# Seven products instead of eight for the first pair of K tiles in a feed-forward, and one low part instead of two

## The chip, the core and the metric

The kernel runs on one core of one Trainium2 chip. The metric is device time of one execution in microseconds (us); the median of three runs is given, with the lowest and highest. A core has five engines that take their own instructions in order: TensorE (PE, matrix products), VectorE (DVE), ScalarE (ACT), GpSimd (POOL, used here only to issue DMAs) and SyncE (SP, which issues most loads). They meet through semaphores: an instruction waits until another engine or a DMA has counted far enough.

## The reference

One block of an encoder, in float32, on 256 tokens of width 2048:

```
x += 1/2 * swiglu(norm(x))         # first feed-forward, inner width 5632
x += gated merge of two recurrent branches of norm(x), through w_out
x += cross attention to 256 memory tokens
x += 1/2 * swiglu(norm(x))         # second feed-forward
return norm(x)

def swiglu(h, w_up, w_down):
    gate, up = split(h @ w_up, 2)
    return (silu(gate) * up) @ w_down
```

The change touches the `h @ w_up` of the first feed-forward, and in one detail that of the second as well. There h is 256 x 2048 and w_up 2048 x 11264; gate and up are its two halves.

## The kernel before, in words

**Split operands.** A float32 matrix product of full accuracy is made of three faster ones. Each operand is split into a high part `h` (the value rounded to the type fp32r, made by ACT with a copy) and a low part `l` (value less high part, made by DVE with a subtraction): function `split`. A product is high times high, low of x times high of w, and high of x times low of w: function `three`, lines 547, 548 and 550. The x operands are the stationary side, 128 x 128; the weights stream past, 512 columns at a time.

**Groups and pairs.** The inner width of a feed-forward is worked through in 11 groups of 512 (g from 0 to 10). In a group the 2048 rows of x and w_up are taken as eight pairs of 128-row K tiles, p from 0 to 7; the weights of one pair are one load of 128 x 2048: two K tiles times gate and up. After the eight pairs the group is evacuated from PSUM (`ev`), multiplied, turned by transposes into `hidop`, and used in a later group by the down products (`wd`, four loads of 128 x 2048 in a group from g = 3 on).

**Seven products.** With two K tiles, two halves of the tokens, and gate and up, a pair is a 2 x 2 by 2 x 2 block product. Written out (kind "plain") it takes eight products of a 128 x 128 block of x with 512 columns of w, each three matmuls. Kind "fast" takes Strassen's scheme in Winograd's form: seven products, 21 matmuls, of sums and differences of blocks. For this the weights need four more blocks, `td`, made by DVE in three operations (L285, L287, L288), and split like the others into `th` and `tl`; x needs four sums as well, made once by `operand_pairs` and kept in the second half of the slots `xh` and `xl`. Kind "mixed" leaves w as it is and puts differences of x in its place: eight products, 24 matmuls, and the results still land in the seven accumulators of "fast". The x differences of "mixed" are the operand `less`. The table `PRODUCTS` lists, for each product, block of x, block of w and accumulator.

**Order.** `ffn_order` writes the order of pairs and down products by hand. From the fourth group on (g of 3 and more) nearly all pairs are fast; p0 is mixed, because the second half of its `xh` and `xl` holds `less` and has no room for the sums. `BOTH` lists those pairs of x that have both `less` and sums; for these, `less` stands in extra tiles, `xd`.

**Preparing weights.** `weights` takes items from the plan two ahead of their use and calls `prepare`, which loads, makes `td`, and splits. For p3 to p6 of groups 4 and up (function `adds`) the low part of the weights is not made by DVE: ACT writes the negated high part source (L293) and POOL issues a DMA that adds the weights to it (L294). Two dictionaries, `head` and `rest`, hang other work behind the preparation of numbered items: the operands of x, residual loads, sums.

**Buffers and scheduler.** Loads have three buffers (`raw`), high parts three (`h`), low parts three (`l`); `td`, `tl` and the evacuated `ev` of the first feed-forward share three of `wide`. The second feed-forward has no such pool for `tl`, two more load buffers, and loads most of its `td` ready-made from HBM, where the middle of the kernel has put them (`make_ahead`, tile `prep`). The order of instructions on each engine comes from a scheduler that places them by its own costs and the program's priorities; `tc.issue_after` binds some of them to a place. So a change in the program can move instructions that it does not name.

Of the kernel before, what the change touches and what calls it, by code (L numbers as in the profile page):

```python
# [8 lines left out]
F32 = mybir.dt.float32  # L9
F32R = mybir.dt.float32r  # L10
ACT = mybir.ActivationFunctionType
ALU = mybir.AluOpType

P = 128
# [27 lines left out]
def ffn_order(every=False):  # L42

    out = [(("mixed" if p > 5 else "fast") if every else "plain", 0, p) for p in range(8)]
    down = [("down", 0, 1, c, 0) for c in range(4)]  # L50
    for g in range(1, NG):
        if every:
            out += [("fast", g, p) for p in (1, 3, 4, 0, 2, 5, 6, 7)]
        elif g < 3:
            out += [(("mixed", "fast")[p % 2], g, p) for p in (0, 1, 2, 3, 5, 4, 7, 6)]
        else:
            out += [("mixed" if p == 0 or g == 3 and p == 6 else "fast", g, p)
                    for p in ((1, 3, 0, 4, 2, 6, 5, 7) if g == 3 else (1, 3, 4, 0, 2, 5, 6, 7))]
        if g > 2 and g % 2:
            down = [("down", g - 2, 2, c, b) for c in range(4) for b in (g - 2, g - 1)]  # L60
        n = 2 if g < 3 else 4
        out, down = out + down[:n], down[n:]
    return out + [("down", NG - 2, 2, c, b) for c in range(4) for b in (NG - 2, NG - 1)]
# [14 lines left out]
def block_kernel(ctx: ExitStack, tc: tile.TileContext, xT, xin, memT, vec, gfin, bgate, lruw, wu1, wd1, win, wv,  # L78
                 wg, wab, wout, wq, wk, wvm, wo, wu2, wd2, out_):
    nc = tc.nc  # L80
    pe, dve, act, sp = nc.tensor, nc.vector, nc.scalar, nc.sync
# [23 lines left out]
    def slot(dt=F32, name="slot"):  # L105
        return slots.tile([P, 1024], dt, name=name, tag="slot")
# [24 lines left out]
    x = [xt[k // 4][:, (k % 4) * T:(k % 4 + 1) * T] for k in range(KT)]  # L131
    ident = col("ident", 0, P)

    done = {}


    def split(h, l, raw):
        done["high"] = act.activation(h, raw, ACT.Copy).ins  # L138
        done["low"] = dve.tensor_tensor(out=l, in0=raw, in1=h.bitcast(F32), op=ALU.subtract).ins  # L139

    def split_tiles():
        return hp.tile([P, 2048], F32R, name="h", tag="h"), lp.tile([P, 2048], F32R, name="l", tag="l")


    plan, ahead, made_ahead = [], [], []
    orders = {"ffn1": ffn_order(), "ffn2": ffn_order(every=True)}

    def plan_ffn(name, wu, wd):
# [41 lines left out]
    head, rest = [], {}  # L190
# [29 lines left out]
    def weights(*key):  # L220
        while plan and len(ahead) < 2:
            i = next(planned)
            k, src, kind = plan.pop(0)
            if i == 0:
                in_turn.enter_context(tc.manual_schedule(engines={sp.engine, act.engine, dve.engine}))
            if i < len(head):
                head[i]()
            if plan and plan[0][2] == "added":
                begun.append(begin_added(plan[0][1]))
            ahead.append((k, prepare(src, kind, 4 if i < 4 else 1)))  # L230
            if i in rest:
                rest[i]()
            beside(i)
            if i == 7:
                in_turn.close()
        k, w = ahead.pop(0)
        assert k == key, (k, key)
        return w
# [4 lines left out]
    def raw_tile():  # L243

        if "raw2" in scoped and next(loads) % 5 > 2:
            return scoped["raw2"].tile([P, 2048], F32, name="raw2", tag="raw2")
        return rawp.tile([P, 2048], F32, name="raw", tag="raw")
# [10 lines left out]
    def prepare(src, kind, cuts=1):  # L258

        if kind == "added":  # L260
            raw, l = begun.pop(0)
            h = hp.tile([P, 2048], F32R, name="h", tag="h")
            done["high"] = act.activation(h, raw, ACT.Copy).ins
            return h, l
        raw = raw_tile()
        n = 2048 // cuts
        if kind == "plain":
            h, l = split_tiles()
            for a in range(0, 2048, n):
                sp.dma_start(raw[:, a:a + n], src[:, a:a + n])  # L270
                split(h[:, a:a + n], l[:, a:a + n], raw[:, a:a + n])
            return h, l
        if kind == "ready":
            src, t = src
            sp.dma_start(raw[:, 512:], src[:, 512:])
            td = raw_tile()
            sp.dma_start(td, t)
        else:
            sp.dma_start(raw, src)
            if "raw2" in scoped:  # L280
                td = raw_tile()
            else:
                td = scoped["wide"].tile([P, 2048], F32, name="td", tag="wide")
            two = [v[:, a:a + 1024].rearrange("p (i n) -> p i n", i=2) for v, a in ((td, 0), (raw, 512))]
            dve.tensor_tensor(out=two[0], in0=raw[:, None, :512].broadcast_to([P, 2, 512]), in1=two[1],  # L285
                              op=ALU.subtract)
            dve.tensor_tensor(out=td[:, 1024:1536], in0=raw[:, 1024:1536], in1=td[:, :512], op=ALU.subtract)  # L287
            dve.tensor_tensor(out=td[:, 1536:], in0=raw[:, 1536:], in1=td[:, 1024:1536], op=ALU.subtract)  # L288
        h, l = split_tiles()
        if kind != "fast added":  # L290
            split(h[:, 512:], l[:, 512:], raw[:, 512:])
        else:
            act.activation(l[:, 512:], raw[:, 512:], ACT.Copy, scale=-1.0)  # L293
            nc.gpsimd.dma_start(l[:, 512:], src[:, 512:], accum_op=ALU.add)  # L294
            done["high"] = act.activation(h[:, 512:], raw[:, 512:], ACT.Copy).ins
        th = hp.tile([P, 2048], F32R, name="h", tag="h")
        if "wide" in scoped:
            tl = scoped["wide"].tile([P, 2048], F32R, name="tl", tag="wide")
        else:
            tl = lp.tile([P, 2048], F32R, name="tl", tag="l")  # L300
        for a in (0, 1024):
            split(th[:, a:a + 1024], tl[:, a:a + 1024], td[:, a:a + 1024])
        return (h, l), (th, tl)

    def product(xs, *ws, late=()):
# [182 lines left out]

    BOTH = [2, 4, 6]
    xd = []

    def operand_pairs(src, gain, q, xg, out, every=False):


        for a in src:
# [8 lines left out]
            if every:  # L506
                less = None
                if q == 3:
                    if not i:
                        xd.append(slot(F32R, "xd"))  # L510
                    less = [xd[-1][:, a:a + 256] for a in (512 * i, 512 * i + 256)]
            elif 2 * q + i in BOTH:
                n = 512 * (BOTH.index(2 * q + i) % 2)
                if not n:
# [4 lines left out]
        def sums(which=((0, "less"), (0, "sums"), (1, "less"), (1, "sums"))):  # L519
            s = slot(name="xs")  # L520
            for i, ((h, l), less) in enumerate(out):
                a = [xg[:, i * 512 + j * P:][:, :P] for j in range(4)]

                def made(h, l, n, at, terms):
                    o = [s[:, at + j * P:][:, :P] for j in range(n)]
                    for j, (x, y, op) in enumerate(terms(o)):
                        dve.tensor_tensor(out=o[j], in0=x, in1=y, op=op)
                    split(h, l, s[:, at:at + n * P])

                if less and (i, "less") in which:  # L530
                    made(*less, 2, 0, lambda o: ((a[0], a[1], ALU.subtract), (a[2], a[3], ALU.subtract)))
                if (every or i or 2 * q in BOTH) and (i, "sums") in which:
                    if not every and not i and len(which) > 1:
# [139 lines left out]
    pairs1, sq1 = [], TokenSquares()  # L673
# [30 lines left out]
    def late_sums(q):  # L704
        with tc.issue_after(done["low"]):
            sums1[q](((0, "sums"),))

    for q, i in ((1, 16), (2, 17), (3, 26)):
        rest[i] = lambda q=q: late_sums(q)


    par = const.tile([P, 96], F32, name="par")
# [56 lines left out]
    xs = xs2.tiles  # L769
# [372 lines left out]
    for g in range(4):  # L1142
# [4 lines left out]
        for t in range(2):  # L1147
            s = slot(F32R, "vs")
# [8 lines left out]
    for h in range(HEADS):  # L1157
        for j in range(4):
            acc = bank()
            for t in range(2):  # L1160
                ps = probs[h][:, t * 512:(t + 1) * 512]
                s = vs[h, t]
# [153 lines left out]
```

## Time and profile before

| | us |
|---|---|
| median of three runs | 2428.28 (2426.31 to 2430.49) |
| span of the profiled execution, first to last instruction | 2425.5 |
| PE busy in the span | 2409.3 (99%) |
| DVE busy | 2025.6 (84%) |
| ACT busy | 1455.0 (60%) |
| DMA | 684.31 MB, mean 282 GB/s |

The own time of the profiled execution isn't among the numbers shown; its span lies 2.8 us below the median, and that is taken as what lies around the span.

How to read the lines that follow. A busy engine is one whose instructions run; on a page, an instruction's line names engine, source line, operation, and tiles as out<-in (partitions x elements). A row of a timeline starts with start and length in us; a bracket at its end tells how long the engine idled before it and what ended that. Matmuls overlap: a row's 0.39 us is longer than the 0.23 from one start to the next. PEld is the load of the stationary side, beside PE.

| from about | to | stage |
|---|---|---|
| 0 | 280 | first feed-forward, groups 0 to 3 |
| 280 | 715 | first feed-forward, groups 4 to 10, and its last down products |
| 715 | 1900 | recurrent branches and cross attention |
| 1900 | 2425 | second feed-forward, last norm |

### The profile page before, as it was taken

The numbers are of one execution on the slowest core, as the hardware profiler recorded it, in microseconds if no ns is written. First come the engines' busy times: TensorE is split into PE (matmuls) and PEld (weight loads), VectorE is DVE, ScalarE is ACT, GpSimd is POOL, SyncE is SP. The second block draws the span as 40 slices with busy tenths as digits, with TensorE's granted clock in tenths as the row PEclk, the third lists the DMA queues.
The fourth block names the chain that finished last, engine by engine and source line by source line (L and its number), as shares of the span: only waits on it lengthen the run. The fifth ranks groups of instructions, "written<-read, shape, count | busy, mean of one in ns | idle before, by whom it ended". The sixth has DMA issues, their size and how long they took to land.

```text
span 2425.5 us, 30763 instructions
## 1 busy us (share of the span) xinstructions
PE 2409.3 (99%) x12139; PEld 2013.6 (83%) x12139; DVE 2025.6 (84%) x2260; ACT 1455.0 (60%) x1485; POOL 102.2 (4%) x166
## 2 busy tenths in 40 slices
PE   9999999999999999999999999999999999999998
PEld 8888888888788888888888888888888788888887
DVE  7999999998876868779776788777789999999995
ACT  8567677777664454476434555445676666666664
POOL 0000000000000000000000000000000000000000
PEclk9999999999999999999999999999999999999999
DMA  7579999988858776778989889977798878787873
GB/s 294 195 229 287 272 272 270 275 269 268 266 183 323 268 289 241 294 289 323 346 313 349 310 332 354 335 272 263 264 343 308 285 266 293 273 286 276 294 273 144
DMA packets 102385, 684.31 MB, mean 282 GB/s; under 512 B 11361, under 2 KB 11617, under 8 KB 29281
## 3 DMA queue, kind: packets, MB, share of 16 engines
q1 hardware_dynamic: 78192, 518.68, 57.5%
q0 software_dynamic: 23328, 162.54, 22.4%
q8 instruction: 95, 1.56, 0.2%
q10 hardware_dynamic: 720, 1.13, 0.1%
q14 instruction: 50, 0.40, 0.0%
HBM read 619.39 MB, written 62.91 MB: 281 GB/s over the span
## 4 chain that ended last, share of the span: by engine, by line
PE 91%; DVE 3%; DMA 3%; ACT 1%; issue 1%; ACTq 0%; DVEq 0%; SPq 0%
PE acc L547 16%; PE acc L548 16%; PE acc L550 16%; PE acc L313 11%; PE acc L338 8%; PE acc L341 8%; PE acc L339 8%; PE acc L316 6%; DMA raw<-wd 2%; DVE tl L139 1%; ACT h L138 1%; DVE l L139 1%; PE acc L588 1%; PE acc L477 1%; DMA t<-prep 0%
## 5 line engine op out<-in xcount | busy, mean ns | idle before, releaser
L138 ACT ACTIVATE h<-raw 128x2048 fp32r<-128x2048 f32 (+3 forms) x578 | 870.5, 1531 | 620.2 <-PE acc L339 189.6
L139 DVE TENSOR_TENSOR l<-raw,h 128x2048 fp32r<-128x2048 f32 (+2 forms) x406 | 837.3, 2065 | 187.6 <-ACT h L138 186.1
L547 PE MATMUL acc<-h,xh 128*128 128x512 f32 x1241 | 485.2, 392 | 2.7 <-ACT h L138 2.4
L548 PE MATMUL acc<-h,xl 128*128 128x512 f32 x1241 | 483.0, 390 | 0.0
L338 PE MATMUL acc<-h,ops 128*128 128x512 f32 x832 | 326.8, 393 | 0.0
L339 PE MATMUL acc<-h,ops 128*128 128x512 f32 x832 | 324.5, 390 | 0.0
L547 PEld LDWEIGHTS acc<-h,xh 128*128 128x128 f32 x1241 | 233.3, 188 | 56.2 <-ACT h L138 8.0
L547 PE MATMUL acc<-h,hidop 128*128 128x512 f32 x704 | 276.5, 393 | 2.3 <-ACT h L138 2.2
L313 PE MATMUL acc<-ops,h 128*128 128x512 f32 x1152 | 278.2, 393 | 0.0
L548 PE MATMUL acc<-h,hidop 128*128 128x512 f32 x704 | 274.8, 390 | 0.0
L548 PEld LDWEIGHTS acc<-h,xl 128*128 128x128 f32 x1241 | 233.3, 188 | 47.5
L313 PEld LDWEIGHTS acc<-ops,h 128*128 128x128 f32 x1152 | 211.7, 188 | 41.6
L139 DVE TENSOR_TENSOR tl<-raw,h 128x1024 fp32r<-128x1024 f32 x172 | 203.7, 1220 | 14.9 <-ACT h L138 14.5
L341 PE MATMUL acc<-l,ops 128*128 128x512 f32 x832 | 205.8, 389 | 0.0
L550 PE MATMUL acc<-l,hidop 128*128 128x512 f32 x704 | 189.3, 389 | 0.0
L138 ACT ACTIVATE h<-td 128x1024 fp32r<-128x1024 f32 x126 | 131.3, 1057 | 92.9 <-PE acc L548 42.3
L341 PEld LDWEIGHTS acc<-l,ops 128*128 128x128 f32 x832 | 156.2, 188 | 32.4
L338 PEld LDWEIGHTS acc<-h,ops 128*128 128x128 f32 x832 | 156.2, 188 | 32.2
L339 PEld LDWEIGHTS acc<-h,ops 128*128 128x128 f32 x832 | 156.3, 188 | 31.5
L139 DVE TENSOR_TENSOR tl<-td,h 128x1024 fp32r<-128x1024 f32 x126 | 152.0, 1220 | 31.2 <-ACT h L138 31.0
L200 DVE TENSOR_TENSOR prep<-prep 128x512 f32<-128x512 f32 x232 | 159.7, 689 | 20.9 <-DMA prep<-wu 17.1
L550 PE MATMUL acc<-l,xh 128*128 128x512 f32 x645 | 176.4, 389 | 0.0
(242 smaller groups left out, 2739.4 us busy)
## 6 DMA issues: line engine op xcount, KB each, us to landing
raw<-wu SPq DMA_DIRECT2D x114, 1024.0 KB, 6.3
raw<-wd SPq DMA_DIRECT2D x88, 1024.0 KB, 6.3
prep<-wu POOLq DMA_DIRECT2D x58, 1024.0 KB, 7.8
t<-prep POOLq DMA_DIRECT2D x58, 1024.0 KB, 7.8
raw<-t SPq DMA_DIRECT2D x58, 1024.0 KB, 6.9
raw<-wu SPq DMA_DIRECT2D x58, 768.0 KB, 5.0
raw<-win SPq DMA_DIRECT2D x40, 1024.0 KB, 4.8
raw<-wg SPq DMA_DIRECT2D x32, 1024.0 KB, 6.1
```

The lines of the kernel that those rows point to most:

```text
L138: done["high"] = act.activation(h, raw, ACT.Copy).ins
L139: done["low"] = dve.tensor_tensor(out=l, in0=raw, in1=h.bitcast(F32), op=ALU.subtract).ins
L200: dve.tensor_tensor(out=b[o], in0=b[x], in1=b[y], op=ALU.subtract)
L313: pe.matmul(acc, h[:, k * P:(k + 1) * P], xs[k], start=k == 0, stop=False)
L316: done["product"] = pe.matmul(acc[:, :T], l[:, k * P:(k + 1) * P], xs[k][:, :T], start=False, stop=k == KT - 1).ins
L338: pe.matmul(accs[t], x[:, t * P:][:, :P], h[j], start=first and j == 0, stop=False)
L339: pe.matmul(accs[t], x[:, T + t * P:][:, :P], h[j], start=False, stop=False)
L341: done["product"] = pe.matmul(accs[t], x[:, t * P:][:, :P], l[j], start=False, stop=last and j == 3).ins
L477: pe.transpose(acc[:, z * T + t * P:][:, :P], tile[:, t * 512 + (2 * y + z) * P:][:, :P], ident)
L547: pe.matmul(acc, ah, bh, start=start, stop=False)
L548: pe.matmul(acc, al, bh, start=False, stop=False)
L550: pe.matmul(acc, ah, bl, start=False, stop=stop)
```

## The change

From the fifth group of the first feed-forward on (g of 4 and more), p0 is of kind "fast" too. `BOTH` gets a 0, so that the `less` of p0 stands in an `xd` tile and the second half of its slots is free. The sums of x for p0 are made by a new function, `first_sums`, behind the preparation of item 33, which lies in the fourth group: it adds high and low part of p0's x to have x back, makes the four sums and splits them. Last, in both feed-forwards, the low part `tl` of a fast product is made by one DVE operation of 2048 columns in place of two of 1024; the high part `th` is still made by ACT in two halves of 1024.

```diff
@@ ffn_order
         else:
-            out += [("mixed" if p == 0 or g == 3 and p == 6 else "fast", g, p)
+            out += [("mixed" if g == 3 and p in (0, 6) else "fast", g, p)
                     for p in ((1, 3, 0, 4, 2, 6, 5, 7) if g == 3 else (1, 3, 4, 0, 2, 5, 6, 7))]
@@ prepare
         for a in (0, 1024):
-            split(th[:, a:a + 1024], tl[:, a:a + 1024], td[:, a:a + 1024])
+            done["high"] = act.activation(th[:, a:a + 1024], td[:, a:a + 1024], ACT.Copy).ins
+        done["low"] = dve.tensor_tensor(out=tl, in0=td, in1=th.bitcast(F32), op=ALU.subtract).ins
         return (h, l), (th, tl)
@@
-    BOTH = [2, 4, 6]
+    BOTH = [0, 2, 4, 6]
@@
+    def first_sums():
+
+        (h, l), _ = pairs1[0]
+        s = slot(name="xs")
+        a, o = ([s[:, n + j * P:][:, :P] for j in range(4)] for n in (0, 512))
+        with tc.issue_after(done["low"]):
+            dve.tensor_tensor(out=s[:, :512], in0=h[:, :512].bitcast(F32), in1=l[:, :512].bitcast(F32), op=ALU.add)
+            for j, (x, y, op) in enumerate(((a[1], a[3], ALU.add), (o[0], a[0], ALU.subtract),
+                                            (a[1], a[0], ALU.subtract), (a[2], o[1], ALU.subtract))):
+                dve.tensor_tensor(out=o[j], in0=x, in1=y, op=op)
+            split(h[:, 512:], l[:, 512:], s[:, 512:])
+
+    rest[33] = first_sums
```

## The prediction

> **What bounds the kernel now.** I read the page's head, then busy time by stage, then three hand-overs on the timelines. First the page, then busy time in one group of the first feed-forward and in two stretches of the second, at its start and inside.
>
> ```profile
> span 2425.5 us, 30763 instructions
> ...
> PE 2409.3 (99%) x12139; PEld 2013.6 (83%) x12139; DVE 2025.6 (84%) x2260; ACT 1455.0 (60%) x1485; POOL 102.2 (4%) x166
> ...
> 342.00:404.00 62.00, 61.96 (x277) 51.08 (x277) 56.60 (x58) 44.25 (x36) 4.60 (x6) 1.00 0.90 271
> ...
> 1900.00:2000.00 100.00, 97.22 (x420) 78.37 (x419) 91.92 (x87) 62.81 (x53) 1.76 (x2) 0.98 0.79 279
> ...
> 2100.00:2200.00 100.00, 100.00 (x449) 82.59 (x449) 90.64 (x87) 64.64 (x56) 1.73 (x2) 1.00 0.81 281
> ```
>
> The columns of the last three rows are stretch, length, then PE, PEld, DVE, ACT and POOL busy, granted clock, DMA share, GB/s. PE is full in both feed-forwards, but for 2.8 us at the second's start; DVE has 5.4 of 62 us left in a group, ACT 17.8. So a matmul less is time less, as long as DVE and ACT still deliver. How near they are shows PE's timeline over a group:
>
> ```profile
> 405.39 0.39 PE L547 MATMUL acc<-h,xh 128*128 128x512 f32 x1
> ...
> 438.71 0.39 PE L547 MATMUL acc<-h,xh 128*128 128x512 f32 x1
> ...
> 440.75 0.39 PE L548 MATMUL acc<-h,xl 128*128 128x512 f32 x1
> ...
> 441.41 0.50 PE L547 MATMUL acc<-h,xh 128*128 128x512 f32 x1
> ...
> 443.62 1.08 PE L550 MATMUL acc<-tl,xh 128*128 128x512 f32 x4
> ...
> 467.19 0.39 PE L547 MATMUL acc<-h,xh 128*128 128x512 f32 x1
> ```
>
> From 438.71 to 440.75 lie nine steps: a matmul costs PE 0.227 us. From 405.39 to 467.19 lies a group: 61.80 us, 267 matmuls and some transposes. I name products p0 to p7 by pair; this group runs p1 p3 p4 p0 p2 p5 p6 p7, then four down products d1 to d4. At 441.41 PE has waited for p7's high part, and at 443.62 it starts p7's `tl`, which DVE ends that instant (442.38 plus 1.22, next fence). So the last product of each group already has no slack.
>
> ```profile
> 406.15 0.68 DVE L662 SCALAR_TENSOR_TENSOR x<-acc,x 128x512 f32<-128x512 f32 x1
> ...
> 410.86 1.22 DVE L285 TENSOR_TENSOR td<-raw 128x1024 f32<-128x1024 f32 x1
> 412.12 0.69 DVE L287 TENSOR_TENSOR td<-raw,td 128x512 f32<-128x512 f32 x1
> 412.85 0.69 DVE L288 TENSOR_TENSOR td<-raw,td 128x512 f32<-128x512 f32 x1
> 413.46 1.22 DVE L139 TENSOR_TENSOR tl<-td,h 128x1024 fp32r<-128x1024 f32 x1
> 414.59 1.22 DVE L285 TENSOR_TENSOR td<-raw 128x1024 f32<-128x1024 f32 x1
> 415.73 1.22 DVE L139 TENSOR_TENSOR tl<-td,h 128x1024 fp32r<-128x1024 f32 x1
> 416.86 2.28 DVE L139 TENSOR_TENSOR l<-raw,h 128x2048 fp32r<-128x2048 f32 x1
> 419.06 0.68 DVE L287 TENSOR_TENSOR td<-raw,td 128x512 f32<-128x512 f32 x1
> 419.67 1.75 DVE L139 TENSOR_TENSOR l<-raw,h 128x1536 fp32r<-128x1536 f32 x1
> 421.34 0.68 DVE L288 TENSOR_TENSOR td<-raw,td 128x512 f32<-128x512 f32 x1
> ...
> 435.04 1.22 DVE L285 TENSOR_TENSOR td<-raw 128x1024 f32<-128x1024 f32 x1
> ...
> 440.18 2.28 DVE L139 TENSOR_TENSOR l<-raw,h 128x2048 fp32r<-128x2048 f32 x1
> 442.38 1.22 DVE L139 TENSOR_TENSOR tl<-td,h 128x1024 fp32r<-128x1024 f32 x1
> ```
>
> Start to start, which is what a queue pays, L285 costs 1.26 before the operation that reads it and 1.13 before another, L287 0.73, L288 0.61, a `tl` half 1.13, a low part of 1536 columns 1.67, of 2048 columns 2.20. From 413.46 to 416.86 one product's halves stand around the next product's L285: that weaving keeps DVE at work while ACT makes a high half. ACT's side, where the halves at 426.72 are together and those of p7 are parted by a down product's high part:
>
> ```profile
> 404.75 1.49 ACT L295 ACTIVATE h<-raw 128x1536 fp32r<-128x1536 f32 x1 [1.99 <-PE acc L548]
> 406.14 1.47 ACT L293 ACTIVATE l<-raw 128x1536 fp32r<-128x1536 f32 x1
> ...
> 426.72 2.01 ACT L138 ACTIVATE h<-td 128x1024 fp32r<-128x1024 f32 x2
> ...
> 436.37 1.06 ACT L138 ACTIVATE h<-td 128x1024 fp32r<-128x1024 f32 x1 [1.13 <-DVE td L285]
> 438.06 1.92 ACT L138 ACTIVATE h<-raw 128x2048 fp32r<-128x2048 f32 x1 [0.62 <-PE acc L548]
> 440.29 1.06 ACT L138 ACTIVATE h<-td 128x1024 fp32r<-128x1024 f32 x1 [0.32 <-DVE td L288]
> 441.26 1.90 ACT L138 ACTIVATE h<-raw 128x2048 fp32r<-128x2048 f32 x1
> ```
>
> A high half costs 0.96 start to start and 1.06 to its end, one of 1536 columns 1.39 and 1.49. ACT starts 0.11 after DVE's L285 ends (435.04 plus 1.22, 436.37).
>
> **The change, part by part.** *Matmuls.* In groups 4 to 10 p0 goes from eight products to seven, three matmuls less: 7 x 3 x 0.227 = 4.8 us, all on the path where PE is the bound. *DVE for it.* p0 took one low part of 2048 columns, 2.20; it now takes 1.26 + 0.73 + 0.61 + 1.67 + 2.20 = 6.47: +4.3 us a group. *ACT for it.* +1.6 us a group; ACT has room.
>
> *One low operation instead of two.* The rows by shape:
>
> ```profile
> L139 DVE TENSOR_TENSOR l<-raw,h 128x2048 fp32r<-128x2048 f32 x269 | 615.3, 2288 | 184.3 <-ACT h L138 182.9 <-DMA xf<-xT 1.1
> L139 DVE TENSOR_TENSOR tl<-td,h 128x1024 fp32r<-128x1024 f32 x126 | 152.0, 1220 | 31.2 <-ACT h L138 31.0
> L285 DVE TENSOR_TENSOR raw<-raw 128x1024 f32<-128x1024 f32 x28 | 34.2, 1220 | 5.2 <-DMA raw<-wu 5.2
> L527 DVE TENSOR_TENSOR xs<-xg 128x128 f32<-128x128 f32 x42 | 10.8, 284 | 0.0
> ```
>
> By duration a pair saves 2 x 1.22 - 2.29 = 0.15 us; on the queue only 2 x 1.13 - 2.20 = 0.06, as neighbours overlap. Eight in a group: 0.5 us. But now DVE can't begin before ACT has made both halves. [...]
>
> *What the schedule makes of it.* In the changed kernel's built order, groups 4 to 10 stand thus (D: L285, L287, L288; tha, thb: the high halves; neg: a negated copy for an accumulating DMA):
>
> ```
> ACT: neg4 tha3 h4 thb3 tha4 h0 thb4 tha0 h2 thb0 neg5 neg6 tha2 h5 thb2 tha5 h6 thb5 tha6 h7 thb6 tha7 hd1 thb7 hd2
> DVE: x x D3 tl3 D4 l0 tl4 D0 l2 tl0 D2 tl2 D5 tl5 D6 l7 tl6 D7 ld1 tl7 ld2
> PE:  tl7 stands behind 180 of the group's 264 matmuls
> ```
>
> ACT makes the next product's high part between two halves in every product; DVE has the whole `tl` ahead of the next L285, and at most one low part to fill the wait. Queues run in order, so each product is one loop: L285, half, other high part, half, `tl`, next L285. With nothing between (p2, p5): 1.22 + 0.11 + 0.96 + 1.39 + 1.06 + 2.20 = 6.9 us. With a low part between, which waits for that other high part (p4, p0, p6): 1.22 + 0.11 + 0.96 + 1.49 + 1.67 + 2.20 = 7.65. p7, with d1 between: 1.22 + 0.11 + 0.96 + 1.91 + 2.20 + 2.29 = 8.7. p3: h4 waits for the buffer of p1's high sums, free at 3.4 after PE's start of the group (14 matmuls at 0.227, the last one's 0.39 less its step, 0.1 for the signal), then 1.39 + 1.06 + 2.20: its `tl` leaves the queue at 8.05. PE needs 21 x 0.227 = 4.8 us a product, so it loses over 2 us on each.
>
> The loop starts late each time: D3 stands behind two residual adds, the second of which needs the last matmul before the group, so it begins near 0.9 (0.3, then an add of 0.68, as at 406.15, less the overlap); p3's L285 fits ahead of 3.4.
>
> One more wait is in SP's queue. p6's weights now load into the buffer that p0's L288 frees, at some 15.7 + 2.6 = 18.3 us into the group, and land after
>
> ```profile
> raw<-wu SPq DMA_DIRECT2D x114, 1024.0 KB, 6.3
> ...
> l<-wu POOLq DMA_DIRECT2D x28, 768.0 KB, 9.9
> ```
>
> 6.3 us, at 24.8; neg6 reads them and stands ahead of p2's first half, which without it could start at 24.7: it starts at 26.3, 1.6 later. POOL's order is unchanged; its accumulating loads take 9.9 us and l5 comes some 2 us after PE wants it, inside what PE waits for DVE anyway.
>
> Sum for a group, from PE's start: 8.05 + 7.65 (p4) + 7.65 (p0) + 6.9 + 1.6 (p2) + 6.9 (p5) + 7.65 (p6) + 8.7 (p7) = 55.1: `tl7` ends there. PE reaches it after 180 x 0.227 = 40.8. It waits 14.3 us in all. Behind it lie 84 matmuls, 19 us, in which DVE has ld2, nine evacuation operations (some 0.6 each, as the add at 406.15) and ld4 to do, some 10, so the downs end on time and the next group begins the same. A group takes 61.8 - 0.7 (matmuls) - 0.3 (the wait at 441.41, counted anew) + 14.3 = 75.1, or 13.3 more; seven groups: 93 us.
>
> [...]
>
> *Sums of x.* One addition, four of 128 columns at 0.28, a split (0.69 DVE, 0.63 ACT) in group 3, about 2.5 us of DVE once, where two products need no DVE: between 0 and +2.5, I take 0. `xd` has the same operations in another tile: 0.
>
> *Elsewhere.* Groups 1 to 3 (14 merged pairs) and the second feed-forward (86) keep nearly their order, with a low part or another product's `tl` between. Lower bound: PE's idle time around the second's start, 2.8 us. Upper: see the third rival. I take 0, as DVE's rows there show 9 us free in 100.
>
> Total: 2425.5 + 93 = 2518 for the profiled execution; the median of the runs shown, 2428.3, lies 2.8 above its span: 2522.
>
> **Rivals.** *PE stays the bound.* If a product's loop fits under 4.8 us, by woven halves, only the matmuls count: 2428.3 - 4.8 = 2423.5, faster by 0.2%. For it speaks PE's 61.96 of 62; it decides as soon as nothing of another product stands between ACT's halves and the next L285 stands ahead of `tl`; the built order has neither. Chance 0.06. *Only DVE's work counts.* If its waits were filled, DVE would need 38 us from D3 to tl7 (seven `tl` 15.4, six later D 15.6, low parts 7.2), from 5.9 (p3's halves) to 44.1, 3.3 after PE: less 0.7 and 0.3, +2.3 a group, 2444. For it: DVE is the busiest after PE. Against: the order leaves nothing to fill them with. Chance 0.08. *The merge also hurts outside groups 4 to 10.* The 28 products of the second feed-forward whose differences DVE makes itself (L285 on `raw`) and 14 of groups 1 to 3 each lose the 1.13 of a half handed over early: +47, 2569. Against: there other low parts fill the time. Chance 0.12. *It does nothing measurable* (gains in the second feed-forward cancel a small loss): 0.03.
>
> **How the numbers follow.** Forecast 0.71. Its bounds: with no low part between and no neg6, `tl7` ends at 8.05 + 6 x 6.9 = 49.5, 8.7 late, +7.7 a group, 2482; with l5's 2 us not hidden, +15.3 a group, 2535. To hold 8 in 10, the range takes in the third rival's weaker half: 2482 to 2560. 0.2% (4.9 us) is about what can be told from no change: faster 0.06, same 0.03, slower 0.91.
>
> **What would show it.** Each group from the fifth on 73 to 77 us long between first matmuls; PE about 12 to 15 us idle in it, mostly for ACT's halves and for `tl`; DVE's idle time before `tl` ended by ACT, over 1 us in p2 and p5; `tl` rows of 2048 columns near 2.29; busy time of PE 4.8 less. The second feed-forward as long as before. Wrong, if a group takes 61 to 65 us, or if the time comes from the second feed-forward.

## The result and the profile after

The changed kernel takes 2527.4 us (median of five runs, 2525.6 to 2528.6) against 2428.3 (2424.6 to 2430.5) on the same chip: 1.041 times as long, with a 95% interval of 1.040 to 1.043. The forecast was 2522, with a range of 2482 to 2560.

First the head of the page after:

```profile
span 2526.8 us, 30672 instructions
...
PE 2443.3 (97%) x12118; PEld 2002.0 (79%) x12118; DVE 2055.5 (81%) x2145; ACT 1460.6 (58%) x1500; POOL 102.2 (4%) x166
```

Then its busy time by stage: a group of the first feed-forward, from its first matmul to the next group's, and two stretches of the second (columns as in the prediction: stretch, length, PE, PEld, DVE, ACT, POOL, granted clock, DMA share, GB/s).

```profile
378.25:453.14 74.89, 65.64 (x274) 48.98 (x272) 61.14 (x55) 44.71 (x39) 4.37 (x5) 1.00 0.74 217
1900.00:2000.00 100.00, 98.58 (x441) 80.97 (x440) 90.35 (x70) 64.30 (x60) 0.00 (x0) 1.00 0.80 311
2100.00:2200.00 100.00, 99.31 (x441) 81.59 (x440) 93.13 (x72) 64.01 (x57) 0.87 (x1) 1.00 0.78 270
```

PE executes 21 matmuls less (12118 for 12139) and takes longer. In the group no engine is full any more: DVE works 61.1 of 74.9 us. (PE's busy time has grown too: a matmul's row is 0.16 us longer than its step, 0.39 for 0.227, and ahead of a wait up to that much of it counts as busy; so the page counts only 9.3 us of this group as idle, where the starts of its matmuls leave 13.8, in 33 gaps.) In the second feed-forward PE is no longer quite full, 99.3 for 100.0.

Where the time lies, by the first transpose of each group on PE (line 588 before, 589 after), from the trace. These transposes come some 6 us ahead of the next group's first matmul, so the first row holds groups 1 to 3 and the second groups 4 to 10:

| us | before | after | difference |
|---|---|---|---|
| from the first group's transposes to the fourth's | 155.5 | 166.8 | +11.3 |
| from there to the eleventh's: seven groups | 434.8 (62.1 each) | 523.3 (74.8 each) | +88.5 |
| to the second feed-forward's first | 1136.1 | 1135.0 | -1.1 |
| to the second feed-forward's last | 582.7 | 585.7 | +3.0 |

The span has grown by 101.3, which these four rows make but for rounding and the ends.

The same group on DVE, after (start, length, then in brackets the idle time before the row and what ended it):

```profile
376.98 2.29 DVE L303 TENSOR_TENSOR tl<-td,h 128x2048 fp32r<-128x2048 f32 x1
379.19 1.28 DVE L663 SCALAR_TENSOR_TENSOR x<-acc,x 128x512 f32<-128x512 f32 x2
380.38 1.22 DVE L285 TENSOR_TENSOR td<-raw 128x1024 f32<-128x1024 f32 x1
...
385.13 2.29 DVE L303 TENSOR_TENSOR tl<-td,h 128x2048 fp32r<-128x2048 f32 x1 [2.08 <-ACT h L302]
387.34 1.22 DVE L285 TENSOR_TENSOR td<-raw 128x1024 f32<-128x1024 f32 x1
...
391.14 1.76 DVE L139 TENSOR_TENSOR l<-raw,h 128x1536 fp32r<-128x1536 f32 x1 [1.13 <-ACT h L138]
392.82 2.28 DVE L303 TENSOR_TENSOR tl<-td,h 128x2048 fp32r<-128x2048 f32 x1
395.02 1.22 DVE L285 TENSOR_TENSOR td<-raw 128x1024 f32<-128x1024 f32 x1
...
402.68 1.22 DVE L285 TENSOR_TENSOR td<-raw 128x1024 f32<-128x1024 f32 x1
...
409.68 1.22 DVE L285 TENSOR_TENSOR td<-raw 128x1024 f32<-128x1024 f32 x1
...
416.62 1.22 DVE L285 TENSOR_TENSOR td<-raw 128x1024 f32<-128x1024 f32 x1
...
424.27 1.22 DVE L285 TENSOR_TENSOR td<-raw 128x1024 f32<-128x1024 f32 x1
...
430.69 2.28 DVE L303 TENSOR_TENSOR tl<-td,h 128x2048 fp32r<-128x2048 f32 x1
```

The starts of L285 are p3, p4, p0, p2, p5, p6 and p7; the last row is p7's `tl`. Before each `tl`, or before the low part that stands ahead of it, DVE idles for a high part of ACT's. ACT in its turn:

```profile
396.33 1.06 ACT L302 ACTIVATE h<-td 128x1024 fp32r<-128x1024 f32 x1 [4.27 <-DVE td L285]
397.30 1.47 ACT L138 ACTIVATE h<-raw 128x1536 fp32r<-128x1536 f32 x1
398.67 1.04 ACT L302 ACTIVATE h<-td 128x1024 fp32r<-128x1024 f32 x1
...
402.68 1.49 ACT L293 ACTIVATE l<-raw 128x1536 fp32r<-128x1536 f32 x1 [1.59 <-DMA raw<-wu]
404.08 1.04 ACT L302 ACTIVATE h<-td 128x1024 fp32r<-128x1024 f32 x1
```

ACT idles 4.27 us for DVE's next L285, makes a half, another product's high part and the second half, and after one more operation idles again, this time 1.59 us for p6's load. The two engines take turns. What PE waits for in the seven groups (total us, times, longest):

```profile
PE acc L548 <- ACT h L302: 35.4, 34, 1.4
PE acc L551 <- DVE tl L303: 11.5, 16, 0.9
PE acc L548 <- ACT h L138: 6.4, 19, 0.6
PE acc L551 <- DMA l<-wu: 2.6, 3, 1.8
PE acc L548 <- ACT h L295: 2.3, 13, 0.2
```

These come in the order in which the loop hands over: first halves, then `tl`. From start to start of its matmuls PE's gaps in the group shown sum to 13.8 us (steps over 0.3 us, less 0.227 each); the list holds 58.2 for seven groups, 8.3 each, as part of each gap, up to 0.16 us, lies in the row of the matmul ahead of it.

### The profile page after: what moved, and what is told of

Its sections match the earlier page's. It is cut to its first block, busy times and chain, and to the rows that moved or that the text cites. A ratio compares the mean times of both kernels' runs of the same rounds, so it can differ in the third digit from the quotient of the medians.

```text
span 2526.8 us, 30672 instructions
## 1 busy us (share of the span) xinstructions
PE 2443.3 (97%) x12118; PEld 2002.0 (79%) x12118; DVE 2055.5 (81%) x2145; ACT 1460.6 (58%) x1500; POOL 102.2 (4%) x166
## 3 DMA queue, kind: packets, MB, share of 16 engines
q10 hardware_dynamic: 720, 1.13, 0.1%
## 4 chain that ended last, share of the span: by engine, by line
PE 77%; DVE 10%; ACT 6%; issue 4%; DMA 3%; SPq 0%; ACTq 0%; DVEq 0%
PE acc L551 12%; PE acc L548 12%; PE acc L549 12%; PE acc L314 11%; PE acc L339 7%; PE acc L342 7%; PE acc L340 7%; PE acc L317 5%; DVE tl L303 4%; DVE l L139 3%; ACT h L138 3%; DVE td L285 2%; DMA raw<-wu 1%; ACT h L302 1%; ACT h L295 1%
## 5 line engine op out<-in xcount | busy, mean ns | idle before, releaser
L138 ACT ACTIVATE h<-raw 128x2048 fp32r<-128x2048 f32 (+2 forms) x406 | 699.1, 1726 | 523.9 <-PE acc L340 186.8
L549 PE MATMUL acc<-h,xl 128*128 128x512 f32 x1228 | 476.3, 393 | 0.0
L302 ACT ACTIVATE h<-raw 128x1024 fp32r<-128x1024 f32 x172 | 174.6, 1054 | 135.7 <-PE acc L549 79.6
L302 ACT ACTIVATE h<-td 128x1024 fp32r<-128x1024 f32 x140 | 147.1, 1051 | 183.4 <-DVE td L285 154.5
L303 DVE TENSOR_TENSOR tl<-raw,h 128x2048 fp32r<-128x2048 f32 x86 | 196.2, 2288 | 30.4 <-ACT h L302 30.2
L303 DVE TENSOR_TENSOR tl<-td,h 128x2048 fp32r<-128x2048 f32 x70 | 160.1, 2288 | 50.4 <-ACT h L302 49.6
L551 PE MATMUL acc<-tl,xh 128*128 128x512 f32 x624 | 174.6, 400 | 17.8 <-DVE tl L303 16.8
```

Of the source, the lines that this page charges most:

```text
L302: done["high"] = act.activation(th[:, a:a + 1024], td[:, a:a + 1024], ACT.Copy).ins
L303: done["low"] = dve.tensor_tensor(out=tl, in0=td, in1=th.bitcast(F32), op=ALU.subtract).ins
L549: pe.matmul(acc, al, bh, start=False, stop=False)
L551: pe.matmul(acc, ah, bl, start=False, stop=stop)
```

## The experiments

All ten runs by the same marks (us; the columns are groups 1 to 3, groups 4 to 10, and the second feed-forward, as in the table above):

| kernel | median | ratio to before, 95% | 1 to 3 | seven | second |
|---|---|---|---|---|---|
| before | 2428.3 | | 155.5 | 434.8 | 582.7 |
| after | 2527.4 | 1.041 (1.040 to 1.043) | 166.8 | 523.3 | 585.7 |
| e1: after, `tl` in halves again | 2473.3 | 1.019 (1.017 to 1.020) | 155.4 | 482.0 | 581.0 |
| e2: before, `tl` in one | 2488.7 | 1.025 (1.024 to 1.027) | 166.3 | 484.2 | 585.3 |
| e3: after, `th` in one too | 2603.2 | 1.073 (1.071 to 1.075) | 180.4 | 553.7 | 610.9 |
| e4: after, halves of `th` together | 2506.5 | 1.034 (1.032 to 1.035) | 166.1 | 490.0 | 595.5 |
| e5: before, `tl` in one in the second | 2427.3 | 1.001 (1.000 to 1.002) | 155.7 | 433.7 | 584.9 |
| e6: e1, p0's low part by DMA | 2439.9 | 1.005 (1.004 to 1.006) | 155.4 | 450.1 | 582.5 |
| e7: e1, p5's source earlier | 2429.7 | 1.002 (1.000 to 1.003) | 155.6 | 438.3 | 582.9 |
| e8: e7, second down part behind p7 | 2426.3 | 1.000 (0.999 to 1.001) | 156.1 | 433.7 | 580.4 |
| e9: e8, p0's low part by DMA | 2438.9 | 1.006 (1.005 to 1.008) | 155.7 | 447.1 | 581.4 |
| e10: e8, `tl` in one again | 2529.7 | 1.043 (1.041 to 1.045) | 166.4 | 523.4 | 584.3 |

Each ratio is to runs of the kernel before on the same chip beside it, whose medians lay between 2425.1 and 2428.3.

**One part undone, one part alone.** e1 puts the halves of `tl` back; e2 is the kernel before with the one operation.

```diff
@@ e1, against after
         for a in (0, 1024):
-            done["high"] = act.activation(th[:, a:a + 1024], td[:, a:a + 1024], ACT.Copy).ins
-        done["low"] = dve.tensor_tensor(out=tl, in0=td, in1=th.bitcast(F32), op=ALU.subtract).ins
+            split(th[:, a:a + 1024], tl[:, a:a + 1024], td[:, a:a + 1024])
@@ e2, against before
         for a in (0, 1024):
-            split(th[:, a:a + 1024], tl[:, a:a + 1024], td[:, a:a + 1024])
+            done["high"] = act.activation(th[:, a:a + 1024], td[:, a:a + 1024], ACT.Copy).ins
+        done["low"] = dve.tensor_tensor(out=tl, in0=td, in1=th.bitcast(F32), op=ALU.subtract).ins
```

> The changed kernel with one thing undone: the low part tl is made by two operations of 1024 columns again; p0 stays a product of seven. In its built order ACT still parts the two high halves by the next product's high part, but DVE has the first half of tl and the next product's L285 ahead of the second half. My theory (the one low operation with the order it brings costs nearly all of the 99 us): the hand-over DVE to ACT to DVE no longer stands alone in the queue, a product costs DVE 1.26 + 1.13 + 0.73 + 0.61 + 1.13 = 4.9 us and 1.67 more with a low part, so DVE is about full and PE waits 0 to 3 us a group: groups of 61 to 64 us, time 2423.5 to 2445, I take 2440. Rival A (p0's added work on DVE, 4.3 us a group, is what costs): groups stay at 70 us and more, 2490 to 2527. The 11 us lost before the fifth group: gone if they are the merge's, still there if they are the sums of x.

> The kernel before with one thing changed: tl in one operation of 2048 columns; p0 stays mixed. Its built order has ACT's halves parted and the whole tl ahead of the next L285, as in the changed kernel, but for p0, which has no differences. My theory, by the same loops, from D4 at 9.1 us after PE's start of the group (read in the changed kernel): p4 8.6 (with p0's low part of 2048 between), p2 6.9, p5 6.9, p6 7.65, p7 8.7, so tl7 ends at 47.9 where PE wants it at 41.5: groups of 67 to 68 us, seven of them +43, with 11 lost in groups 2 to 4 and 2 in the second feed-forward some 2484 (2465 to 2495). Rival A (p0's DVE work costs): 2425 to 2435. Rival B (the merge hurts in the second feed-forward): that stage grows by over 10 us.

e2 came out as my theory had it: +61.6 us, its loops on DVE 6.96, 8.64, 7.92, 6.96, 7.65 and 8.69 us where 8.6 (p4), 6.9, 6.9, 7.65 and 8.7 were expected for those from p4 on (p2's 7.92 has a low part of 1536 columns in it that the sum left out). It also settles groups 1 to 3: their 11 us are the merge's (166.3, as after), and the sums of x cost nothing (e1: 155.4, as before). e1 did not come out: 2473, not 2440, 46 us above before, and rival A's 2490 wasn't reached either. The list of PE's waits in its seven groups has nearly one entry:

```profile
PE acc L550 <- DMA l<-wu: 33.8, 9, 5.3
PE acc L550 <- DVE tl L139: 1.2, 4, 0.3
```

And PE's timeline around one of them, in e1:

```profile
522.63 0.40 PE L548 MATMUL acc<-h,xl 128*128 128x512 f32 x1
527.79 1.22 PE L550 MATMUL acc<-l,xh 128*128 128x512 f32 x2 [4.76 <-DMA l<-wu]
...
530.09 0.63 PE L547 MATMUL acc<-h,xh 128*128 128x512 f32 x1
530.52 0.63 PE L548 MATMUL acc<-h,xl 128*128 128x512 f32 x1
...
532.50 0.39 PE L547 MATMUL acc<-h,xh 128*128 128x512 f32 x1
```

Once a group PE waits 4.2 to 5.3 us for p5's low part, which an accumulating DMA makes, and the matmuls behind it take 0.43 from start to start instead of 0.227 until 532.2. Together that is about the 7 us by which e1's groups are longer than those of before. The transfer is late because its source stands late on ACT:

```profile
513.18 1.07 ACT L138 ACTIVATE h<-td 128x1024 fp32r<-128x1024 f32 x1 [1.29 <-DVE td L285]
514.28 1.49 ACT L295 ACTIVATE h<-raw 128x1536 fp32r<-128x1536 f32 x1
515.68 2.84 ACT L293 ACTIVATE l<-raw 128x1536 fp32r<-128x1536 f32 x2
```

The sources of p5 and p6 (L293) stand behind p2's first half, which waits 1.29 us for p2's L285 on DVE; and that comes later now, as p0's differences stand ahead of it.

**Is it the parting of the halves on ACT?** e3 makes the high part in one operation, e4 binds the next product's high part behind both halves.

```diff
@@ e3, against after
-        for a in (0, 1024):
-            done["high"] = act.activation(th[:, a:a + 1024], td[:, a:a + 1024], ACT.Copy).ins
-        done["low"] = dve.tensor_tensor(out=tl, in0=td, in1=th.bitcast(F32), op=ALU.subtract).ins
+        split(th, tl, td)
@@ e4, against after
-        if kind != "fast added":
-            split(h[:, 512:], l[:, 512:], raw[:, 512:])
-        else:
+        if kind == "fast added":
             act.activation(l[:, 512:], raw[:, 512:], ACT.Copy, scale=-1.0)
             nc.gpsimd.dma_start(l[:, 512:], src[:, 512:], accum_op=ALU.add)
+        with tc.issue_after(done["high"]):
             done["high"] = act.activation(h[:, 512:], raw[:, 512:], ACT.Copy).ins
+        if kind != "fast added":
+            done["low"] = dve.tensor_tensor(out=l[:, 512:], in0=raw[:, 512:], in1=h[:, 512:].bitcast(F32),
+                                            op=ALU.subtract).ins
```

> The changed kernel with the high part th in one operation of 2048 columns as well, so that nothing parts ACT's halves. But one high operation needs all three differences. My theory (what costs is the hand-over that stands alone in two queues that run in order, not the parting): loop of a product 1.26 + 0.73 + 0.69 + 0.11 + 1.91 + 2.20 = 6.9 us, with a low part in front of the differences 8.6, so tl7 ends near 55 us into the group again: groups of 73 to 76 us, time 2510 to 2535. Rival C (the parting of the halves by 1.39 us is what costs): seven times 1.4 us less a group, groups near 66 us, 2460.

> The changed kernel with the next product's high part bound behind both high halves of the product before, so that nothing parts the halves; tl stays one operation. In its built order the whole tl still stands ahead of the next L285, and ld1 and ld2 (2.2 us each) now stand ahead of tl7. My theory (every product is one loop through both queues): a product without a low part 1.22 + 0.11 + 0.96 + 1.06 + 2.20 = 5.55 us, with one 6.5, p7 with three low parts 11; from D3 at 2.1 us tl7 ends at 48.7 where PE asks at 40.8: groups of 68 to 70 us, 7 x 6 less than the changed kernel: 2485 (2470 to 2500). If the parting of the halves were all of the merge's cost, the groups would come down to the 64 to 65 us that DVE's amount of work allows: 2455. If it had no part in it: 2527.

Starts of L285 on DVE in one group of e3:

```profile
483.22 1.22 DVE L285 TENSOR_TENSOR td<-raw 128x1024 f32<-128x1024 f32 x1
487.95 2.29 DVE L139 TENSOR_TENSOR tl<-td,h 128x2048 fp32r<-128x2048 f32 x1 [2.06 <-ACT h L138]
490.16 1.22 DVE L285 TENSOR_TENSOR td<-raw 128x1024 f32<-128x1024 f32 x1
...
497.10 1.22 DVE L285 TENSOR_TENSOR td<-raw 128x1024 f32<-128x1024 f32 x1
...
505.58 1.22 DVE L285 TENSOR_TENSOR td<-raw 128x1024 f32<-128x1024 f32 x1
```

Its loops are the expected ones, 6.94 and 8.48, and nothing parts the halves any more: rival C's 2460 did not come, for e3 is the slowest of all. But the one high operation also waits for all three differences, so e4 is the cleaner test of the parting. I expected the groups no longer than after, and they are 79.1: PE waits up to 2.6 us at a time here, and stretches of matmuls at half clock follow in every group (the mean granted clock from 316 to 792 us is 0.95). I had also left out what the same loop does elsewhere: groups 1 to 3 grow by 25 us over before and the second feed-forward by 28.

e4's groups are 70.0, where 68 to 70 was expected, so the parting, with what else that binding moved, is worth 33 of the 88 us, and the loop with the halves together still costs 55. A loop without a low part is 6.0 us in it (L285 at 441.32, 447.32 and 453.34), where I had put 5.55: the second half reads what L288 writes, 1.26 + 0.73 + 0.69 behind the start of L285, so with nothing in between ACT has to wait for that. The time, 2506 for 2485, was missed by 9 us in the seven groups (33 gained where 42 were expected), by 10 in the second feed-forward, where the same binding took hold, and by 2 between.

**The late transfer.** e7 is e1 with p5's load and negated source put ahead of p2's halves; e6 is e1 with p0 among the pairs whose low part comes by DMA.

```diff
@@ e7, against e1: preparing p2
             split(h[:, 512:], l[:, 512:], raw[:, 512:])
+            if plan and plan[0][2] == "fast added" and plan[0][0][-1] == 5:
+                raw5, l5 = raw_tile(), lp.tile([P, 2048], F32R, name="l", tag="l")
+                sp.dma_start(raw5, plan[0][1])
+                neg = act.activation(l5[:, 512:], raw5[:, 512:], ACT.Copy, scale=-1.0).ins
+                nc.gpsimd.dma_start(l5[:, 512:], plan[0][1][:, 512:], accum_op=ALU.add)
+                begun.append((raw5, l5))
...
         for a in (0, 1024):
-            split(th[:, a:a + 1024], tl[:, a:a + 1024], td[:, a:a + 1024])
+            with tc.issue_after(neg) if neg else nullcontext():
+                split(th[:, a:a + 1024], tl[:, a:a + 1024], td[:, a:a + 1024])
@@ e6, against e1
-    return name == "ffn1" and e[0] == "fast" and e[1] > 3 and e[2] in (3, 4, 5, 6)
+    return name == "ffn1" and e[0] == "fast" and e[1] > 3 and e[2] in (0, 3, 4, 5, 6)
```

> The run with two halves of tl and p0 of seven products, and in groups 4 to 10 p5's load and the negated source of its low part (ACT, L293) put ahead of p2's high halves in ACT's queue; nothing else is changed. In the run without it PE waited once a group, 4.4 to 5.4 us, for the accumulating DMA of p5's low part, and its clock was halved behind that for 2 to 4 us. Theory D (that transfer, started late because its source stands in ACT's queue behind p2's first half, which waits for DVE, is what p0's extra DVE work costs): the source is ready about 3.8 us earlier, the wait falls under 1.5 us and the halved clock goes: groups of 62 to 64 us, 2473 less 7 x 5.5 = 2434 (2426 to 2445). Rival (DVE's amount of work itself, 60.3 us busy in a group): PE waits for tl or high halves instead, 2455 to 2473.

> As the run with two halves of tl and p0 of seven products, and p0's low part of 1536 columns taken from DVE: ACT writes the negated high part's source and POOL issues an accumulating DMA, as for p3 to p6. DVE has 1.67 us less a group, ACT 1.39 more. My theory (with the halves back DVE's amount of work is what is left over): 7 times up to 1.67 less than that run, so 2424 to 2433, and no less than 2423.5, the floor by PE's 147 matmuls saved. Rival (queues and waits, not DVE's amount): no better than that run, or slower, as the transfer takes 10 us and ACT has one operation more.

e7 settles it. Moving one operation of ACT, 1.48 us long, with the load that it reads, takes 43.6 us off e1. PE's waits in its seven groups:

```profile
PE acc L562 <- ACT h L138: 4.1, 5, 1.5
PE acc L565 <- DMA l<-wu: 1.0, 2, 0.5
PE acc L565 <- DVE tl L139: 0.4, 1, 0.4
```

The wait for the transfer has gone from 33.8 us to 1.0, and the granted clock, which was 0.50 for 34.1 us in e1's seven groups, is full in all of e7's (0.999 over its whole span). So it was not the amount of DVE's work that cost. e6 missed its 2424 to 2433 (2439.9; the 147 matmuls in its expectation should be 21). Still it gained 33 us, more than the 12 that 1.67 us of DVE a group could give: its built order has p5's source ahead of p2's halves as well, so it changed two things, and alone it shows nothing of DVE's share.

**What is left.** In two groups of e7 PE lost 1.7 us, in a third 0.9 (the expectation below says 1.7 in three): ACT waited for a down product's load with p7's second half behind it. e8 binds that high part behind the half; e9 is e8 with p0's low part by DMA, as in e6.

```diff
@@ e8, against e7: preparing a down product
+            last = done["halves"].pop(0) if done.get("halves") else None
             for a in range(0, 2048, n):
                 sp.dma_start(raw[:, a:a + n], src[:, a:a + n])
-                split(h[:, a:a + n], l[:, a:a + n], raw[:, a:a + n])
+                with tc.issue_after(last) if last else nullcontext():
+                    split(h[:, a:a + n], l[:, a:a + n], raw[:, a:a + n])
...
+        if "wide" in scoped:
+            done["halves"] = [None, done["high"]]
```

> The run with p5's negated source put early, and in the first feed-forward the high part of a group's second down product bound behind p7's second high half in ACT's queue. In the run without it three groups of the seven lost 1.7 us where ACT waited for that down product's load with p7's half behind it, the others 0.3 to 0.9. Theory: those waits go, groups of 61.1 to 62 us, 2429.7 less some 6: 2423.5 (2420 to 2428), the floor by PE's matmuls. Rival: p7's half is late by DVE's differences as well, the wait only changes its name: 2427 to 2431.

> As the run with the second down product's high part bound, and p0's low part by an accumulating DMA as well (1.67 us a group less on DVE, 1.39 more on ACT, 0.77 MB more to move). If DVE's amount of work still costs something in the run without it: up to 5 us less, 2419 at least. If the order of the queues is what counts: no better, or worse by the order that comes with it, as p0's low part by DMA brings p2's and p4's halves behind more work of ACT: 2425 to 2440.

By the medians e8 is 3.4 us faster than e7, and it is level with the kernel before. One of its groups:

```profile
399.80:460.70 60.90, 60.90 (x273) 50.28 (x272) 59.34 (x63) 45.99 (x39) 4.37 (x5) 1.00 0.89 269
```

PE is full for 60.9 us, 0.9 less than a group of before, with DVE at work for 59.3 of them. The seven groups hold 433.7, 1.1 less than before. The rest of the 4.8 that the matmuls are worth goes into groups of up to 62.8; two waits of 1.0 and 1.2 us for an accumulating DMA are part of it. e9 is 12.6 us worse than e8, with 7.2 us of waits for the accumulating DMA and 7.0 for high halves: relieving DVE through ACT and the DMA queue loses here.

**The merge, on the mended order, and in the second feed-forward.** e10 is e8 with the low part in one operation (the edit of e2); e5 is the kernel before with it in the second feed-forward alone.

> The run with p5's negated source early and the second down product's high part bound, which is no slower than before, with one thing changed: tl in one operation of 2048 columns again. Theory (loops): the built order has the seven loops of the changed kernel again, 7.0 + 7.7 + 7.7 + 7.0 + 6.9 + 7.7 + 8.7 with p3's first; groups of 73.5 to 76 us, 2510 to 2530, so the early source is worth nothing here and the merge alone takes back all. Rival (the costs of the two parts add up, 61 for the merge and 46 for p0, and p0's is mended): 2480 to 2490.

> The kernel before with tl in one operation in the second feed-forward alone. My theory: that stage grows by the 2 to 4 us by which it is longer in both kernels with the merge, and nothing else changes: 2429 to 2432. Rival (its DVE rows gain 86 x 0.06 = 5 us or more, as the merge saves queue time): 2422 to 2427. Rival B of before (it hurts there by tens of us): over 2440.

e10 takes 2529.7: 103 us more than e8 by that one edit, 89.7 of them in the seven groups, and the mended order is worth nothing under it. So the costs of the two parts don't add, although 61.6 (e2) and 46.1 (e1) come near the 99 measured: e1's 46 was the late transfer, and in the changed kernel that transfer is hidden behind what PE waits for anyway. What p0 costs under the merge is a loop of its own: groups of 74.8 us with it, 69.2 without (e2). e5 can't be told from before. The stage itself is 2.2 us longer; the 5 us that 86 times 0.06 on the queue promise are not there.

**Order or size?** The changed kernel holds one more comparison. In groups 1 to 10 a `tl` never stands between a product's L285 and its L288 (0 of the 69 counted); in its second feed-forward, where the merge costs 3 us, one does in 19 of the 28 products whose differences DVE makes, and in e8's seven groups in 44 of the 55 counted. First a hand-over of group 2, then one of the second feed-forward:

```profile
124.76 2.29 DVE L303 TENSOR_TENSOR tl<-td,h 128x2048 fp32r<-128x2048 f32 x1
126.96 1.22 DVE L285 TENSOR_TENSOR td<-raw 128x1024 f32<-128x1024 f32 x1
...
2108.60 1.23 DVE L285 TENSOR_TENSOR raw<-raw 128x1024 f32<-128x1024 f32 x1 [0.96 <-DMA raw<-wu]
2109.74 2.29 DVE L303 TENSOR_TENSOR tl<-raw,h 128x2048 fp32r<-128x2048 f32 x1
```

That speaks for the order and against the size of the operation. It is no proof: no run keeps the one operation in groups 4 to 10 and binds it behind the next L285.

## Why the prediction was right

*PE's matmul, and what p0 saves.* Twenty-one matmuls less were executed. (In the kernel before a matmul of 256 columns on fp32r parts takes 0.120 us from start to start, L316; one on float32 operands as they are, L983, takes two records of 0.216 each.) Their time became visible only in e8, as a group of 60.9 us for 61.8.

*The loops.* Point by point, predicted and measured from the starts of L285 above: p4 7.65 and 7.68 (387.34 to 395.02), p0 7.65 and 7.66, p5 6.9 and 6.94, p6 7.65 and 7.65, p7 to the end of its `tl` 8.7 and 8.70. p7's `tl` ends at 432.97, 54.7 us after PE's start of the group; 55.1 was the sum.

*Two terms were off and cancelled, which is luck.* p3's `tl` left the queue at 9.1, not 8.05 (387.34 less 378.25): D3 began at 2.1, not 0.9, since p1's own `tl`, late by the same loop, ended only at 379.27, one us into the group, with two residual adds behind it. The term for D3 had left p1's `tl` out. The wait for the buffer of p1's high sums, which the text had put on p3's path, isn't there: h4 starts at 382.68 without idle time, right behind the first half, so p3 is an ordinary loop of 6.96. And p2's 1.6 us for the negated source didn't appear (by the text's own 18.3 and 6.3 it would be 1.4): p6's load, issued at 397.75, landed in 4.8 us for the 6.3 reckoned, and p2's L285 came a us late with the rest. The source ended at 404.17, when L285 had just ended at 403.90. p2 took 7.0, not 8.5.

*Groups.* 74.8 on the mean for 75.1, so 88.5 us in seven for 93. Most of the signs named are there: groups of 73.8 to 76.0, PE 13.8 us idle in one, mostly for ACT's halves and `tl`, 2.08 us of DVE's idle time ahead of a `tl` with no low part before it (385.13; 2.12 and 2.06 in p2 and p5), and `tl` rows of 2.28 to 2.29. Two are not: PE's busy time is 34.0 us more, not 4.8 less, as it takes in part of the waits, and the second feed-forward is 3.0 longer.

*Elsewhere 0* was the step that failed. Groups 1 to 3 cost 11.3 and the second feed-forward 3.0, and e2 has nearly the same numbers, 10.8 and 2.6, with nothing but the merge. The text's reason, that the order stays nearly the same and other low parts fill the time, holds in the second feed-forward and not in groups 1 to 3. There the whole `tl` stands ahead of the next L285 as in the later groups (124.76 above), and PE waits for high halves up to 1.7 us at a time:

```profile
PE acc L548 <- ACT h L302: 3.9, 3, 1.7
PE acc L548 <- ACT h L138: 2.1, 4, 0.6
```

So the third rival was true for a third of its 47 us: 0.8 us for each of 14 products in groups 1 to 3, 0.1 for each of 28 in the second feed-forward, where it had 1.13 for all. The misses, -4.5 in the groups and +13 elsewhere (11.3 + 3.0 - 1.1), make the span 2526.8 for 2518; the median lies 0.6 above it, where 2.8 had been added (the profiled execution itself took 2528.6, 1.8 more than its span; and 2518 and 2.8 make 2521, not the 2522 written), so the forecast came out 5 short. That it came so near is partly these misses of opposite sign.

*The rivals.* "Only DVE's work counts" is out: e8 has p0's work on DVE, 59.3 us of 60.9, and costs nothing. "PE stays the bound" is what e8 comes near: PE is full in one group, but the kernel is level with before and not 4.8 us faster. Its condition was put too strictly: in e8 ACT's halves are still parted in most products, with the next L285 (line 290 there) ahead of the second half of `tl`:

```profile
426.78 1.22 DVE L139 TENSOR_TENSOR tl<-td,h 128x1024 fp32r<-128x1024 f32 x1
427.91 1.22 DVE L290 TENSOR_TENSOR td<-raw 128x1024 f32<-128x1024 f32 x1
429.05 1.22 DVE L139 TENSOR_TENSOR tl<-td,h 128x1024 fp32r<-128x1024 f32 x1
```

So the order on DVE was enough there. l5's "2 us, inside what PE waits for DVE anyway" was right for the changed kernel (2.6 us in three waits) and hid the largest surprise, as the cover was gone in e1 and the lateness was then 5 us, not 2.

*Two operations or one.* Here two are right: e10 less e8 is the price of one, 103 us; and in the second feed-forward, where DVE is as busy (90.6 to 93.1 us in each 100 from 1900 to 2300 before) and its other work fills the time, merging gave nothing either (e5).

## What to carry to other kernels

In these kernels two engines that hand a product back and forth had its latency as their period, 6.9 to 8.7 us a product where PE's 21 matmuls take 4.8, wherever the last hand-over stood ahead of the next product's first operation in one of the queues; halving the pieces seems to matter less for the pieces than for what the scheduler can put between them (the two hand-overs above speak for it, no run separates them), so read the built order and not the operation count. Before an engine's amount of work is blamed, look at what PE waits for in the kernel that has only that work: here 46 us were one transfer whose source stood behind an unrelated wait. A wait that is hidden behind another is still a price, due when the other one is mended: PE's waits for low parts by DMA in the seven groups were 2.6 us in the changed kernel and 33.8 in e1.

## What was not expected of the hardware

In these traces 3.41 us of matmuls at half PE's clock followed some waits of about 2 us. In the kernel before, at the start of the second feed-forward, PE's matmuls, and below them the row of the stretch, whose granted clock is 0.50:

```profile
1920.41 0.50 PE L547 MATMUL acc<-h,hidop 128*128 128x512 f32 x1 [2.04 <-ACT h L138]
...
1921.48 0.63 PE L547 MATMUL acc<-h,hidop 128*128 128x512 f32 x1
1921.91 0.63 PE L547 MATMUL acc<-h,xh 128*128 128x512 f32 x1
...
1921.50:1924.80 3.30, 3.30 (x9) 2.63 (x8) 3.30 (x3) 3.30 (x2) 0.00 (x0) 0.50 0.63 191
```

Matmuls go from 0.227 to 0.43 us apart, mostly for seven or eight of them, 1.4 to 1.6 us lost each time. In e6 two waits of 0.69 and 1.12 us within 3.1 us were followed by it too; in e1 it came behind each of the seven long waits, in e3 twenty-three times behind waits of about 2 to 2.7. The changed kernel's waits, mostly below 1.3 us and several us apart, were followed by it four times in the first feed-forward. By the granted clock the slow stretch is 3.41 us each time, or in five cases 6.83.

Why one wait of 2 us is followed by it and another isn't, the traces show in part. Within a trace (its last microseconds left out) the slow stretches start whole multiples of 3.41 us apart: in the changed kernel at 257.03, 270.68, 577.88 and 618.84 us, which is 4, 94 and 106 times 3.413 behind the first. I cut the traces of the kernel before and the changed kernel into windows on that grid and counted idle time from the starts of matmuls, as in the gaps above (steps over 0.3 us, less 0.227 each). The five windows that half clock followed held the most, 2.07 to 2.33 us; of the others none held more than 2.04. That a wait within one window counts in full, while the same wait split over two may not, is my reading of this: no run moved a wait against this grid to test it.
